# Decoder trunk on one core: part of the odd layer's input product split by token halves around the last layer norm of the even layer

## The chip, the cores and the metric

One core of a Trainium2 chip runs the whole kernel. The metric is device time in microseconds (us) of one execution. Three runs of the kernel before gave 1377.31, 1377.62 and 1377.97 us, a median of 1377.62.

## The reference

A trunk of two layers over 256 tokens of width 2048. The even layer has an SSD mixer and a block attention side by side; the odd layer is a diagonal state-space mixer (S5). After each layer the residual is normalised. What matters here is the seam between the two:

```python
x = layer_norm(DEEPNORM_ALPHA * x + h, ln_g[0], ln_b[0])   # h: output projection of the even layer
u, gate = jnp.split(x @ w_in, 2, axis=-1)                  # odd layer: 2048 -> 4096
```

Every row (token) of `x` is normalised over its 2048 features, scaled by `ln_g` and shifted by `ln_b`, and then multiplied by the input weights `in1_w` of the odd layer. All data is float32.

## The kernel before, in words

**Weights as a stream of units.** All large weight matrices are laid out as *units* of 128 partitions x 2 x 512 (256 rows of the matrix by 512 columns, 512 KB). `split_to(i)` brings units in order up to number `i`: SP issues the load of `raw`, ScalarE copies it to a rounded high part `wh` (L224), VectorE subtracts to get the low part `wl` (L226). `raw`, `wh` and `wl` have four buffers each, so a unit's split waits until the unit four places earlier has been multiplied. A product of float32 accuracy is made of three matmuls: high by high, high by low, low by high.

**Two kinds of product.** In the kind "x" (`xmm`, L264) the activations, 128 features by 128 tokens, are the stationary operand and 512 columns of weights move; the result has tokens on partitions. In the kind "w" (`wmm`, L277) 128 x 128 of weights are stationary and the activations of all 256 tokens move; the result has features on partitions. A unit of kind "w" is 2 x 4 x 3 = 24 matmuls. A product over 2048 features has eight units (`CU`), and its sums lie in two PSUM banks that `banks()` hands out in turn from two pairs.

**The even layer's output projection** is four blocks of 512 columns with 16 units each. The last block uses `product_apart`: ten units for both token halves, then the last six (`NKEEP`), whose split weights are all kept in SBUF, first for token half 0 and then for token half 1, 36 matmuls each. So half 0 is complete while PE works on half 1, and its residual and norm (`after0`) run beside that.

**The norm.** For a token half `t`, `res0` adds the residual (L950) and takes statistics (L951); `norm_stats` aggregates them (L967 to L970, with a square root on ScalarE). `step(t, i)` then handles a quarter of the features (512): two VectorE row operations (L993 and L996) give the normalised values `D`; four PE transposes (L341, `transpose4`) turn them into an auxiliary PSUM bank; ScalarE evicts the high part into tile C (L1004) and VectorE the low part into tile F (L1005). C and F are the moving operands of the odd layer's input product. Inside them the 256 token columns lie as four strips of 64, and token half `t` is 32 columns of each strip.

**Order.** A tile scheduler orders each engine's instructions when the program is built, and each engine then takes its instructions in that order; `tc.issue_after` pins an instruction behind another. `jobs` is a queue of small pieces of work that `pump` and `drain` hand out between units. In the kernel before, PE's order at the seam is: 36 matmuls for half 1; eight transposes of steps (0, 0) and (0, 1); 60 dummy matmuls of 128 x 64 by 64 columns on zeros (`warm(WARM1)`, L349); four transposes of step (1, 0); then the first input product `first1`, unit by unit, with 256 moving columns. Step (1, 1), the second quarter of half 1, is handed out before unit 1; the third quarters before unit 3; the last ones before unit 5 (`later`). VectorE's order has the low part of step (1, 0) before the row operations of the later steps, and most of those before the low parts of the later steps.

After this, seven more blocks of the input product follow on PE, beside the state-space mixer; then the GLU product, the output projection and the last norm.

Of the kernel before, what the change touches and what calls it, by code (L numbers as in the profile page):

```python
# [10 lines left out]
F32R = mybir.dt.float32r  # L11
AF = mybir.ActivationFunctionType
OP = mybir.AluOpType
# [3 lines left out]
P = 128  # L17
S = 256
D = 2048
KT = D // P  # L20
UK = 2
CU = KT // UK
ALPHA = 4.0 ** 0.25
NKEEP = 6
WARM0 = 70
WARM1 = 60
EPS = 1e-5
NEG = -1e30
SCALE = 128.0 ** -0.5
# [129 lines left out]
def trunk(tc, io, out):  # L159
    nc = tc.nc  # L160
    V, A, G, T = nc.vector, nc.scalar, nc.gpsimd, nc.tensor
# [6 lines left out]
    with ExitStack() as top:  # L168
# [18 lines left out]
        ident = C("ident")  # L187
# [4 lines left out]
        def big(tag, shape, dt=F32):  # L192
            return slot.tile(shape, dt, tag=tag, name=nm(tag))
# [4 lines left out]
        ready = {}  # L198
# [31 lines left out]
        jobs = deque()  # L230
        back = deque()
        goal = [0, 0.0]
        unit = [0]
# [12 lines left out]
        def drain():  # L246
            while jobs:
                jobs.popleft()()
# [6 lines left out]
        def banks():  # L255
            turnno[0] += 1
            return [main.tile([P, 512], F32, tag=f"m{turnno[0] % 2}{o}", name=nm("main")) for o in range(2)]

        def xmm(ps, o, wpair, j, hk, start, stop):
            (xh, xl), k = hk  # L260
            wh, wl = wpair
            sl = slice(o * P, o * P + P)
            for i, (l, r) in enumerate(((xh, wh), (xh, wl), (xl, wh))):
                T.matmul(ps[o], l[:, k, sl], r[:, j, :], start=start and i == 0, stop=stop and i == 2)  # L264

        def wmm(ps, u, nu, hl, wpair):
            pv = [p.rearrange("p (f n) -> p f n", n=S) for p in ps]
            wh, wl = wpair
            steps = [(j, o) for j in range(UK) for o in range(4)]
            if u == nu - 1:  # L270
                steps = [(j, o) for o in range(4) for j in range(UK)]
            for j, o in steps:
                first, end = u == 0 and j == 0, u == nu - 1 and j == UK - 1
                (xh, xl), k = hl(u * UK + j)
                sl = slice(o * P, o * P + P)
                for i, (l, r) in enumerate(((wh, xh), (wh, xl), (wl, xh))):
                    T.matmul(pv[o // 2][:, o % 2, :], l[:, j, sl], r[:, k, :],  # L277
                             start=first and i == 0 and o % 2 == 0, stop=end and i == 2 and o % 2 == 1,
                             skip_group_check=True)

        def product(kind, hl, nu=CU, prelude=None):
            ps = banks()
            for u in range(nu):
                if prelude:
                    prelude(u)
                split_to(unit[0] + 3)
                wpair = ready.pop(unit[0])
                if kind == "w":
                    wmm(ps, u, nu, hl, wpair)
                else:  # L290
                    last = u == nu - 1
                    steps = [(j, o) for o in range(2) for j in range(UK)] if last else [(j, o) for j in range(UK) for o in range(2)]
                    for j, o in steps:
                        xmm(ps, o, wpair, j, hl(u * UK + j), u == 0 and j == 0, last and j == UK - 1)
                unit[0] += 1
                pump(nu - 1 - u)
            return ps
# [12 lines left out]
                if lo == 0:  # L310
                    between()

        def product_apart(hl, nu, nk, after):
            ps = banks()
            for u in range(nu - nk):
                split_to(unit[0] + 3 + u)
                wpair = ready.pop(unit[0])
                for j in range(UK):
                    for o in range(2):
                        xmm(ps, o, wpair, j, hl(u * UK + j), u == 0 and j == 0, False)  # L320
                unit[0] += 1
                pump(nu - nk - 1 - u)
            drain()
            base = unit[0]
            for o in range(2):
                for i in range(nk):
                    split_to(base + i + 3)
                    u = nu - nk + i
                    for j in range(UK):
                        xmm(ps, o, ready[base + i], j, hl(u * UK + j), u == 0 and j == 0, u == nu - 1 and j == UK - 1)  # L330
                    pump(nk - 1 - i)
                after(ps, o)
                if o == 0:
                    drain()
            for i in range(nk):
                ready.pop(base + i)
            unit[0] += nk

        def transpose4(dst, srcs):
            for i, s in enumerate(srcs):  # L340
                T.transpose(dst[:, i * P : i * P + P], s, ident)  # L341

        idle = cst.tile([P, 64], F32R, name="idle")
        G.memset(idle.bitcast(F32), 0.0)
# [1 line left out]
        def warm(n):  # L346
            px = aux()
            for i in range(n):
                T.matmul(px[:64, 0:64], idle, idle, start=i == 0, stop=i == n - 1)  # L349
# [5 lines left out]
        mr0 = cst.tile([P, 2, 4], F32, name="mr0")  # L355
# [7 lines left out]
        with ExitStack() as l0:  # L363
# [136 lines left out]
            ps = product("w", xhl)  # L500
# [465 lines left out]
        def norm_stats(stt, mr, t):  # L966
            V.bn_aggr(mr[:, t, 0:2], stt[:, t, :, :].rearrange("p a b -> p (a b)"))  # L967
            V.tensor_scalar(mr[:, t, 2:3], mr[:, t, 1:2], EPS, None, op0=OP.add)
            A.activation(mr[:, t, 2:3], mr[:, t, 2:3], AF.Sqrt)
            return lambda: V.reciprocal(mr[:, t, 2:3], mr[:, t, 2:3])  # L970

        with ExitStack() as lt:
            tp = lt.enter_context(tc.tile_pool(name="tp", bufs=1))
            keep[0], keep[1] = tp, range(unit[0] + 2 * CU - NKEEP, unit[0] + 2 * CU)
            rows = [tp.tile([P, D], F32, name=f"row{i}") for i in range(2)]
            for i in range(2):
                nc.sync.dma_start(rows[i], lnrow(i))
            jobs.append(lambda ps=ps: res0(tp.tile([P, 2, 512], F32, tag="xr", name="xr2"), ps, 2, (0, 1)))
            x1n = x1[0]
            x1t = {}  # L980

            tail = {}

            def step(t, i, stats=None):
                if not x1t:
                    x1t["h"] = big("C", [P, KT, S], F32R)
                    x1t["l"] = big("F", [P, KT, S], F32R)
                sl = slice(512 * i, 512 * i + 512)
                xv = x1n[:, t, sl]
                with ExitStack() as pin:  # L990
                    if tail:
                        pin.enter_context(tc.issue_after(tail["v"].ins))
                    V.scalar_tensor_tensor(xv, xv, mr0[:, t, 0:1], rows[0][:, sl], op0=OP.subtract, op1=OP.mult)  # L993
                    if stats:
                        stats()
                    op2 = V.scalar_tensor_tensor(xv, xv, mr0[:, t, 2:3], rows[1][:, sl], op0=OP.mult, op1=OP.add)  # L996
                tail["v"] = op2
                px = aux()
                transpose4(px, [x1n[:, t, (4 * i + f) * P : (4 * i + f) * P + P] for f in range(4)])
                pv = px.rearrange("p (f c s) -> p f s c", f=4, s=4)  # L1000
                fs = slice(4 * i, 4 * i + 4)
                hv = x1t["h"][:, fs, :].rearrange("p f (s c) -> p f s c", s=4)[:, :, :, 32 * t : 32 * t + 32]
                lv = x1t["l"][:, fs, :].rearrange("p f (s c) -> p f s c", s=4)[:, :, :, 32 * t : 32 * t + 32]
                A.activation(hv, pv, AF.Copy)  # L1004
                low = V.tensor_tensor(lv, pv, hv.bitcast(F32), op=OP.subtract)  # L1005
                if (t, i) in ((0, 1), (1, 0)):
                    tail["v"] = low

            def after0(ps, t):
                def first():  # L1010
                    with ExitStack() as pin:
                        if tail:
                            pin.enter_context(tc.issue_after(tail["v"].ins))
                        res0(tp.tile([P, 2, 512], F32, tag="xr", name=nm("xr")), ps, 3, (t,))
                    step(t, 0, norm_stats(st0, mr0, t))

                jobs.append(first)
                if t == 0:
                    jobs.append(lambda: step(0, 1))

            product_apart(tailhl, 2 * CU, NKEEP, after0)
            warm(WARM1)
            drain()
            x1 = x1n

            def x1hl(k):
                return (x1t["h"], x1t["l"]), k

            later = {1: [(1, 1)], 3: [(0, 2), (1, 2)], 5: [(0, 3), (1, 3)]}
            first1 = product("w", x1hl, prelude=lambda u: [step(t, i) for t, i in later.get(u, [])])  # L1030

        ax.close()

# [249 lines left out]
```

## Time and profile before

| | us |
|---|---|
| runs (3) | 1377.31, 1377.62, 1377.97 |
| profiled execution, its own time | 1377.72 |
| its span, first to last instruction | 1375.6 |
| PE busy in the span | 1356.2 |
| mean granted TensorE clock | 0.996 of full |
| SP's and POOL's DMA, whole span | 283.14 MB, mean 206 GB/s |
| last wide matmul of the even layer starts | 865.78 |
| first matmul of the odd layer starts | 873.30 |

How to read it: times inside a profile count from the first instruction of the span. PE is TensorE's matmuls and PEld its weight loads, which overlap with matmuls; DVE is VectorE, ACT ScalarE, POOL GpSimd, SP the engine that issues most DMAs. A timeline row has the start, the duration, the engine, the line, the operation, the tiles (out<-in), the shape of the stationary operand (partitions*columns), of the moving one, and the number of instructions merged in the row; the time in brackets is how long the engine had been idle, and who ended that. Ends of matmuls are modelled, so the pace of a stream is read from starts. In a windows row stand the stretch, its length, the busy time of PE, PEld, DVE, ACT and POOL with counts, the granted clock, the DMA share and GB/s.

### The profile page before, as it was taken

How to read it: one execution, taken by the hardware profiler on the slowest of the kernel's cores; microseconds unless marked ns; L12 is line 12 of the kernel's file. 1: busy time of each engine (PE TensorE's matmuls, PEld its weight loads, DVE VectorE, ACT ScalarE, POOL GpSimd, SP SyncE). 2: the span in 40 equal slices, each digit the busy share in tenths (PEclk: the TensorE clock that was granted, in tenths of full speed). 3: DMA queues.
4: the chain of work that ended last, by engine and by line, in shares of the span. 5: the costliest groups of instructions: out<-in, count | busy, mean ns of one | idle time of the engine just before them, and what ended most of it. 6: DMA issues, size and time to landing. Idle time of an engine off the chain costs nothing.

```text
span 1375.6 us, 27155 instructions
## 1 busy us (share of the span) xinstructions
PE 1356.2 (99%) x11064; PEld 1273.4 (93%) x11064; DVE 981.8 (71%) x1556; ACT 679.5 (49%) x872; POOL 306.2 (22%) x457
## 2 busy tenths in 40 slices
PE   9999999999999999999999999999999999999996
PEld 9999999988998998998988888899999999999885
DVE  5789958777767688687768756758788846454556
ACT  5565468765544544554554435244345545444441
POOL 0258776842011011011000000023433100000001
PEclk9999999999999999999999999999999999999998
DMA  8546665445556656657656669488888665555762
GB/s 306 176 150 190 211 203 189 159 149 192 171 158 201 205 177 210 213 165 228 221 184 222 224 211 323 159 254 275 283 275 277 197 203 183 182 182 182 253 208 86
DMA packets 79212, 283.14 MB, mean 206 GB/s; under 512 B 9840, under 2 KB 10480, under 8 KB 78576
## 3 DMA queue, kind: packets, MB, share of 16 engines
q1 hardware_dynamic: 68112, 239.33, 53.8%
q0 software_dynamic: 10400, 40.90, 9.1%
q8 instruction: 86, 1.41, 0.4%
q10 hardware_dynamic: 576, 1.18, 0.2%
q14 instruction: 38, 0.31, 0.1%
HBM read 260.41 MB, written 20.97 MB: 205 GB/s over the span
## 4 chain that ended last, share of the span: by engine, by line
PE 82%; POOL 10%; DMA 3%; DVE 2%; issue 1%; ACT 1%; POOLq 0%; SPq 0%; ACTq 0%
PE main L277 50%; PE main L264 26%; POOL F L611 5%; DMA wb<-F 2%; POOL F L613 2%; POOL F L614 2%; POOL F L606 1%; PE enc L1093 1%; PE aux L677 1%; PE aux L341 1%; PE aux L349 1%; PE dec L1138 1%; PE aux L673 1%; PE aux L851 1%; PE aux L883 1%
## 5 line engine op out<-in xcount | busy, mean ns | idle before, releaser
L226 DVE TENSOR_TENSOR wl<-raw,wh 128x1024 fp32r<-128x1024 f32 x431 | 538.9, 1255 | 281.9 <-ACT wh L224 275.7
L224 ACT ACTIVATE wh<-raw 128x1024 fp32r<-128x1024 f32 x431 | 454.7, 1058 | 535.8 <-PE main L277 325.5
L277 PE MATMUL main<-A,wl 128*128 128x256 f32 x1920 | 545.5, 284 | 3.7 <-DVE wl L226 3.6
L277 PE MATMUL main<-A,wh 128*128 128x256 f32 x1920 | 548.4, 286 | 0.0
L277 PE MATMUL main<-B,wh 128*128 128x256 f32 x1920 | 544.4, 284 | 0.0
L277 PEld LDWEIGHTS main<-A,wl 128*128 128x128 f32 x1920 | 369.0, 192 | 4.6 <-DVE wl L226 4.5
L277 PEld LDWEIGHTS main<-A,wh 128*128 128x128 f32 x1920 | 369.2, 192 | 0.8 <-issue 0.2
L277 PEld LDWEIGHTS main<-B,wh 128*128 128x128 f32 x1920 | 369.3, 192 | 0.3
L277 PE MATMUL main<-C,wh 128*128 128x256 f32 x512 | 148.1, 291 | 0.7 <-ACT C L1004 0.7
L277 PE MATMUL main<-F,wh 128*128 128x256 f32 x512 | 145.4, 285 | 0.1
L277 PE MATMUL main<-C,wl 128*128 128x256 f32 x512 | 145.1, 284 | 0.0
L277 PEld LDWEIGHTS main<-C,wh 128*128 128x128 f32 x512 | 98.3, 192 | 2.9 <-ACT C L1004 0.9
L264 PE MATMUL main<-wh,A 128*128 128x512 f32 x256 | 100.7, 393 | 0.0
L264 PE MATMUL main<-wl,A 128*128 128x512 f32 x256 | 100.1, 391 | 0.0
L264 PE MATMUL main<-wh,C 128*128 128x512 f32 x256 | 100.0, 392 | 0.0
L264 PE MATMUL main<-wh,B 128*128 128x512 f32 x256 | 99.9, 390 | 0.0
L264 PE MATMUL main<-wl,C 128*128 128x512 f32 x256 | 99.8, 390 | 0.0
L264 PE MATMUL main<-wh,F 128*128 128x512 f32 x256 | 99.8, 390 | 0.0
L277 PEld LDWEIGHTS main<-F,wh 128*128 128x128 f32 x512 | 98.7, 193 | 0.4 <-DVE F L1005 0.4
L277 PEld LDWEIGHTS main<-C,wl 128*128 128x128 f32 x512 | 98.7, 193 | 0.1
L611 POOL TENSOR_TENSOR F<-F 128x16 f32<-128x16 f32 (+5 forms) x96 | 67.1, 720 | 3.8
L685 POOL DMA_DIRECT2D wb<-ob x16 | 8.8, 547 | 254.2 <-ACT ob L678 200.3
(279 smaller groups left out, 1565.2 us busy)
## 6 DMA issues: line engine op xcount, KB each, us to landing
raw<-in_wi SPq DMA_DIRECT2D x271, 512.0 KB, 4.2
raw<-in_wo SPq DMA_DIRECT2D x96, 512.0 KB, 4.2
raw<-in_wglu SPq DMA_DIRECT2D x64, 512.0 KB, 3.5
wt<-wb POOLq DMA_DIRECT2D x16, 896.0 KB, 7.6
wb<-ob POOLq DMA_DIRECT2D x16, 512.0 KB, 4.4
bc<-in_s5bc SPq DMA_DIRECT2D x16, 256.0 KB, 4.4
wb<-F POOLq DMA_DIRECT2D x16, 256.0 KB, 3.8
wb<-om POOLq DMA_DIRECT2D x16, 128.0 KB, 4.2
```

Source lines behind the costliest of these rows:

```text
L224: last["a"] = A.activation(wh, raw, AF.Copy)
L226: last["v"] = V.tensor_tensor(wl, raw, wh.bitcast(F32), op=OP.subtract)
L264: T.matmul(ps[o], l[:, k, sl], r[:, j, :], start=start and i == 0, stop=stop and i == 2)
L277: T.matmul(pv[o // 2][:, o % 2, :], l[:, j, sl], r[:, k, :], start=first and i == 0 and o % 2 == 0, stop=end and i == 2 and o % 2 == 1, sk ...
L341: T.transpose(dst[:, i * P : i * P + P], s, ident)
L349: T.matmul(px[:64, 0:64], idle, idle, start=i == 0, stop=i == n - 1)
L606: G.tensor_copy(cs[:, i, :, 1], phi[:, i, sl])
L611: G.tensor_tensor(pq[:, i, :, :, 0:m], cs[:, :, :, 1 : m + 1], cs[:, i, :, n : n + 1].unsqueeze(1).to_broadcast([P, 2, 8, m]), op=OP.mult)
L613: G.tensor_tensor(cs[:, 0, :, n + 1 : n + 1 + m], pq[:, 0, 0, :, 0:m], pq[:, 1, 1, :, 0:m], op=OP.subtract)
L614: G.tensor_tensor(cs[:, 1, :, n + 1 : n + 1 + m], pq[:, 0, 1, :, 0:m], pq[:, 1, 0, :, 0:m], op=OP.add)
L673: T.transpose(pe[:, a * P : a * P + P], ev[:, a, :], ident)
L677: T.matmul(pk[at : at + 64, a * 16 : a * 16 + 16], ev[:, a, 64 * i : 64 * i + 64], cv[:, a, i, :], start=True, stop=True)
```

## The change

The dummy matmuls at the seam go. `wmm` gets a parameter `t`: with it, a unit is multiplied by the 128 tokens of half `t` alone, so that the moving operand and the result are 4 x 32 columns. After `product_apart` the first three units (`HEAD1`) of the first input product are multiplied by half 0. Only then are the remaining jobs, with residual and norm of half 1, handed out; `first1` then multiplies the same three units by half 1 and the other five by all 256 tokens, into the same two banks. `step` is cut in two: `scaled` (the two row operations) and `turned` (transposes and evictions). `after0` hands out only the `scaled` parts of half 0; their `turned` parts are issued by `mid`, and the last six matmuls of half 1 of `product_apart` (those of the sixth kept unit) are pinned behind its last transpose. For half 1, the first `scaled` part and `turned(1, 0)` are handed out after the head; the other steps stay where they were.

In the issue order of the changed program PE has: 30 of the 36 matmuls for half 1; the eight transposes of half 0; the other six; 72 matmuls of 128 x 128 by 4 x 32 columns (the head); four transposes of step (1, 0); 72 such matmuls for half 1, with the transposes of step (1, 1) after the sixth of unit 1, those of (0, 2) before unit 2, those of (1, 2) and the first of (0, 3) after the first two matmuls of unit 2; then unit 3 with 256 columns, and the remaining transposes behind unit 4. On VectorE, between the low part of (1, 0) and that of (1, 1) stand seven row operations, the split of unit 4 and two row operations; before, it was nine row operations and that split. SP and POOL issue the same instructions in the same order.

```diff
-WARM1 = 60
+HEAD1 = 3
...
-        def wmm(ps, u, nu, hl, wpair):
+        def wmm(ps, u, nu, hl, wpair, t=None):
             pv = [p.rearrange("p (f n) -> p f n", n=S) for p in ps]
+
+            def part(x):
+                return x if t is None else x.rearrange("p (s c) -> p s c", s=4)[:, :, 32 * t : 32 * t + 32]
+
...
-                    T.matmul(pv[o // 2][:, o % 2, :], l[:, j, sl], r[:, k, :],
-                             start=first and i == 0 and o % 2 == 0, stop=end and i == 2 and o % 2 == 1,
+                    T.matmul(part(pv[o // 2][:, o % 2, :]), l[:, j, sl], part(r[:, k, :]),
+                             start=first and i == 0 and o % 2 == 0 and t != 1, stop=end and i == 2 and o % 2 == 1,
                              skip_group_check=True)
...
-        def product(kind, hl, nu=CU, prelude=None):
-            ps = banks()
+        def product(kind, hl, nu=CU, prelude=None, ps=None, head=0):
+            ps = ps or banks()
...
-                    wmm(ps, u, nu, hl, wpair)
+                    wmm(ps, u, nu, hl, wpair, 1 if u < head else None)
...
-        def product_apart(hl, nu, nk, after):
+        def product_apart(hl, nu, nk, after, mid=None):
...
-                    for j in range(UK):
-                        xmm(ps, o, ready[base + i], j, hl(u * UK + j), u == 0 and j == 0, u == nu - 1 and j == UK - 1)
+                    with ExitStack() as pin:
+                        if mid and o == 1 and i == nk - 1:
+                            pin.enter_context(tc.issue_after(mid().ins))
+                        for j in range(UK):
+                            xmm(ps, o, ready[base + i], j, hl(u * UK + j), u == 0 and j == 0, u == nu - 1 and j == UK - 1)
...
-                    step(t, 0, norm_stats(st0, mr0, t))
+                    scaled(t, 0, norm_stats(st0, mr0, t))
 
                 jobs.append(first)
-                if t == 0:
-                    jobs.append(lambda: step(0, 1))
-
-            product_apart(tailhl, 2 * CU, NKEEP, after0)
-            warm(WARM1)
+                jobs.append((lambda: turned(1, 0)) if t else (lambda: scaled(0, 1)))
+
+            def mid():
+                turned(0, 0)
+                return turned(0, 1)
...
+            product_apart(tailhl, 2 * CU, NKEEP, after0, mid)
+            ps = banks()
+            split_to(unit[0] + 3)
+            for u in range(HEAD1):
+                wmm(ps, u, CU, x1hl, ready[unit[0] + u], 0)
             drain()
...
-            first1 = product("w", x1hl, prelude=lambda u: [step(t, i) for t, i in later.get(u, [])])
+            first1 = product("w", x1hl, prelude=lambda u: [step(t, i) for t, i in later.get(u, [])], ps=ps, head=HEAD1)
```

`transpose4` now returns its last transpose; `scaled` and `turned` together hold the lines of `step` unchanged.

More of the change, by code (lines that the diff above doesn't have):

```diff
@@ L340, in transpose4 @@
             for i, s in enumerate(srcs):
-                T.transpose(dst[:, i * P : i * P + P], s, ident)
+                end = T.transpose(dst[:, i * P : i * P + P], s, ident)
+            return end
         idle = cst.tile([P, 64], F32R, name="idle")
@@ L982, in trunk, with scaled @@
             tail = {}
[L984 to L987, printed above, removed]
+            def scaled(t, i, stats=None):
                 sl = slice(512 * i, 512 * i + 512)
@@ L995, in step, with turned @@
                         stats()
-                    op2 = V.scalar_tensor_tensor(xv, xv, mr0[:, t, 2:3], rows[1][:, sl], op0=OP.mult, op1=OP.add)
-                tail["v"] = op2
+                    tail["v"] = V.scalar_tensor_tensor(xv, xv, mr0[:, t, 2:3], rows[1][:, sl], op0=OP.mult, op1=OP.add)
+            def turned(t, i):
+                if not x1t:
+                    x1t["h"] = big("C", [P, KT, S], F32R)
+                    x1t["l"] = big("F", [P, KT, S], F32R)
                 px = aux()
-                transpose4(px, [x1n[:, t, (4 * i + f) * P : (4 * i + f) * P + P] for f in range(4)])
+                end = transpose4(px, [x1n[:, t, (4 * i + f) * P : (4 * i + f) * P + P] for f in range(4)])
                 pv = px.rearrange("p (f c s) -> p f s c", f=4, s=4)
@@ L1007, in step @@
                     tail["v"] = low
+                return end
+            def step(t, i):
+                scaled(t, i)
+                turned(t, i)
             def after0(ps, t):
@@ L1014, in first, with x1hl @@
                         res0(tp.tile([P, 2, 512], F32, tag="xr", name=nm("xr")), ps, 3, (t,))
-                    step(t, 0, norm_stats(st0, mr0, t))
+                    scaled(t, 0, norm_stats(st0, mr0, t))
                 jobs.append(first)
-                if t == 0:
-                    jobs.append(lambda: step(0, 1))
-            product_apart(tailhl, 2 * CU, NKEEP, after0)
-            warm(WARM1)
+                jobs.append((lambda: turned(1, 0)) if t else (lambda: scaled(0, 1)))
+            def mid():
+                turned(0, 0)
+                return turned(0, 1)
+            def x1hl(k):
+                return (x1t["h"], x1t["l"]), k
+            product_apart(tailhl, 2 * CU, NKEEP, after0, mid)
[3 more added lines that the diff above has]
+                wmm(ps, u, CU, x1hl, ready[unit[0] + u], 0)
             drain()
             x1 = x1n
-            def x1hl(k):
-                return (x1t["h"], x1t["l"]), k
             later = {1: [(1, 1)], 3: [(0, 2), (1, 2)], 5: [(0, 3), (1, 3)]}
-            first1 = product("w", x1hl, prelude=lambda u: [step(t, i) for t, i in later.get(u, [])])
+            first1 = product("w", x1hl, prelude=lambda u: [step(t, i) for t, i in later.get(u, [])], ps=ps, head=HEAD1)
         ax.close()
```

## The prediction

> **What bounds the kernel now.** I read the page first, then the chain of work that ended last in order of time, then the PE timeline around the layer norm between the layers. All times are microseconds from the span's start; line numbers are those of the kernel before.
>
> ```profile
> span 1375.6 us, 27155 instructions
> PE 1356.2 (99%) x11064; PEld 1273.4 (93%) x11064; DVE 981.8 (71%) x1556; ACT 679.5 (49%) x872; POOL 306.2 (22%) x457
> PE 82%; POOL 10%; DMA 3%; DVE 2%; issue 1%; ACT 1%; POOLq 0%; SPq 0%; ACTq 0%
> ```
>
> TensorE is the bound. The chain shows where it is not:
>
> ```profile
> 867.28 1.29 DVE F L1005 x2
> 871.15 0.76 DVE D L996
> 874.03 4.40 PE main L277 x24
> 883.04 8.39 PE main L277 x70
> ...
> 1366.08 2.19 DVE D L1256 x3
> ```
>
> At the layer norm the chain leaves PE for DVE, and from 874.03 it stays on PE until 1366. So what delays PE here delays the end by as much, and what is saved is saved. The PE timeline of this stretch:
>
> ```profile
> 865.78 0.39 PE L264 MATMUL main<-wh,B 128*128 128x512 f32 x1
> 866.02 1.03 PE L341 MATMUL aux<-consts,D 128*128 128x128 f32 x8
> 866.81 3.72 PE L349 MATMUL aux<-idle 128*64 128x64 f32 x60
> 871.96 0.66 PE L341 MATMUL aux<-consts,D 128*128 128x128 f32 x4 [1.44 <-DVE D L996]
> 873.30 0.62 PE L277 MATMUL main<-C,wh 128*128 128x256 f32 x2 [0.69 <-ACT C L1004]
> 874.03 0.58 PE L277 MATMUL main<-F,wh 128*128 128x256 f32 x1
> 874.41 0.42 PE L277 MATMUL main<-C,wl 128*128 128x256 f32 x1
> ...
> 877.20 0.28 PE L277 MATMUL main<-C,wl 128*128 128x256 f32 x1
> ...
> 878.14 0.28 PE L277 MATMUL main<-F,wh 128*128 128x256 f32 x1
> ...
> 882.80 0.36 PE L277 MATMUL main<-F,wh 128*128 128x256 f32 x1
> 883.00 0.28 PE L277 MATMUL main<-C,wl 128*128 128x256 f32 x1
> ```
>
> The last useful matmul starts at 865.78 and the next at 873.30: 7.5 us with twelve transposes and sixty dummy matmuls. Starts, not durations, give the pace, since neighbours overlap: eight steps from 877.20 to 878.14 are 118 ns each; at 874.41 a matmul took twice that. The windows view says why (the column after POOL is the granted clock):
>
> ```profile
> 870.00:872.00 2.00, 0.56 (x10) 0.45 (x8) 1.83 (x5) 0.20 (x1) 0.00 (x0) 1.00 0.00 0
> 872.00:874.00 2.00, 1.24 (x6) 0.70 (x6) 0.72 (x2) 0.60 (x1) 0.00 (x0) 0.88 0.00 0
> 874.00:877.00 3.00, 2.97 (x14) 2.98 (x15) 2.93 (x5) 0.00 (x0) 0.00 (x0) 0.51 0.00 0
> 877.00:882.00 5.00, 5.00 (x45) 5.00 (x45) 4.93 (x7) 2.09 (x3) 0.00 (x0) 1.00 0.01 3
> ```
>
> The clock was half for about 3.4 us (0.48 us before 874 and 2.94 after). Some 2.8 us at half pace lost about 1.4 us. In all, before, unit 3 begins at 883.00 + 21 x 0.12 = 885.5 (the 22 left of unit 2 run from 882.80). That is the mark I compare with.
>
> **The change part by part.** It puts 72 matmuls of 128 columns (units 0 to 2, first token half) where the dummies were, and turns the 72 later ones of 256 columns into 72 of 128. The question is what a matmul of 128 columns costs. No row shows this one, so I look at weight loads:
>
> ```profile
> L349 PEld LDWEIGHTS aux<-idle x130: 137/227/227, 0.9 to 870.3; 128*64 128x64 f32 x130
> L692 PEld LDWEIGHTS aux<-kt,consts x48: 187/192/192, 458.9 to 816.8; 128*128 128x128 f32 x48
> 459.06 0.83 PE L692 MATMUL aux<-kt,consts 128*128 128x128 f32 x6
> 459.64 0.36 PE L277 MATMUL main<-A,wh 128*128 128x256 f32 x1
> 459.84 0.28 PE L277 MATMUL main<-B,wh 128*128 128x256 f32 x1
> 817.16 49.02 PE main L264 x216
> ```
>
> A 64-column load takes 137 ns, a 128-column one 192: 55 ns per 64 columns, so 110 ns of loading per full matmul beside a fixed part that overlaps. The dummies agree: sixty from 866.81, the last at 870.3, are 59 ns each for 64 weight columns and only 64 moving ones, and twice 59 is 118. Six of L692, 128 by 128, take (459.84 - 0.12 - 459.06) / 6 = 110 ns. So pace is set by the 128 weight columns as long as few columns move: **110 ns** (L692) to **120 ns** (the 256-column matmul when DMAs run) per half-width matmul. I take 118, the 256-column row, because it has the same operands, weights and DMA-quiet stretch. The far end on the cheap side is a line through 227 ns for 512 columns (49.02 / 216) and 120 for 256: 67 ns for 128; that is a rival below. That the moving part is four strips of 32 columns I cost at nothing: moving 128 columns needs some 53 ns by that line's slope, so even at twice that it hides under the load; without that cover it would add 72 x 2 times the excess.
>
> The other rows that the walk needs:
>
> ```profile
> 863.69 0.75 DVE L996 SCALAR_TENSOR_TENSOR D<-D,mr,row 128x512 f32<-128x512 f32 x1
> 868.49 0.68 DVE L950 SCALAR_TENSOR_TENSOR D<-xr,main 128x512 f32<-128x512 f32 x1
> 873.28 0.69 DVE L1005 TENSOR_TENSOR F<-aux,C 128x512 fp32r<-128x512 f32 x1 [1.38 <-ACT C L1004]
> 873.89 0.74 DVE L993 SCALAR_TENSOR_TENSOR D<-D,mr,row 128x512 f32<-128x512 f32 x1
> 879.02 0.75 DVE L996 SCALAR_TENSOR_TENSOR D<-D,mr,row 128x512 f32<-128x512 f32 x1
> 880.35 1.22 DVE L226 TENSOR_TENSOR wl<-raw,wh 128x1024 fp32r<-128x1024 f32 x1
> 881.48 0.69 DVE L1005 TENSOR_TENSOR F<-aux,C 128x512 fp32r<-128x512 f32 x1
> ```
>
> Transposes of the first half, now ahead of the last six wide matmuls: PE reaches them at 866.02 - 6 x 0.227 = 864.66, and their input is ready at 863.69 + 0.75 = 864.44, so nothing waits. The eight take about 0.87 (8 x 0.109, from 1.03 for eight with one 0.27 tail). The six wide ones then end where the transposes ended: the head starts at **866.9**. Its low parts are ready: L1005 began 1.26 after the transposes (867.28 against 866.02), so the first is done by 866.6. Gain: the eviction hides under matmuls.
>
> Second half's residual and norm on DVE: they follow those two L1005, so they move 1.3 us earlier, from 868.49 to about 867.2. The added wait of L950 on the last wide matmul (about 867.1) costs nothing beside that; behind it are only the norm's own operations. The scaled rows end about 870.6 in place of 871.9. **This gain goes nowhere**, since in the changed issue order their transposes stand behind the whole head on PE, whose queue is in order: 866.9 + 72 x 0.118 = **875.4** (T). Before, it was 871.96.
>
> From T the old chain repeats: evictions, then the third matmul 2.07 after T (874.03 - 871.96), DVE's next row operation 1.93 after T (873.89). The DVE order in the changed program: seven row operations (873.89 to 879.02, 5.13), L226 for unit 4 (881.48 - 880.35 = 1.13), two row operations (880.35 - 879.02 = 1.33), then the low part that unit 2's third matmul needs (0.69). It is there at T + 1.93 + 5.13 + 1.13 + 1.33 + 0.69 + 0.06 = T + 10.3. PE gets to it sooner: 2.07 + 48 x 0.118 + 13 transposes x 0.109 = T + 9.2, so it waits 1.1. The other 22 of unit 2 take 2.6, and unit 3 begins at T + 12.9 = **888.3**. Three transposes that before had been done by then remain: 0.33.
>
> Sum: 888.3 + 0.33 - 885.5 = **+3.1 us**. The second pass costs as much as the old full one, and the first pass is 8.5 us in a gap that had 5.1 left for it. Each nanosecond of pace moves it by 0.094 us (72 + 22 matmuls): +2.3 at 110, +3.3 at 120. The regained clock (1.4) is in it.
>
> Costed at nothing: the sixty dummies go into the head's place; SP and POOL issue the same transfers in the same order, and the weights of the first units lie ready (all queues quiet here, 0 to 3 GB/s in the windows rows); the accumulators taken earlier are the pair idle since the block before; ACT's split of unit 4 waits for unit 0's second pass (about T + 5) and L226 comes at T + 7, so two microseconds cover it. If that cover went, L226 and the low part behind it would be late one for one.
>
> Made against the profiled execution, 1377.72 (span 1375.6 plus 2.1 around it; the median of the runs is 1377.62): 1377.72 + 3.1 = **1380.8**.
>
> **Rivals.**
> *Gate closes once.* PE is idle for 0.9 and 0.5 after T and for 1.1 before unit 2. Before, a window with 0.56 + 1.24 busy in 4 us closed the clock; here the window round the late wait is two thirds busy. Price as before: some 1.4, so 1382.2. The Trainium skill ("TensorE: Matmul & The Clock Gate", section "What's actually happening") says that about one idle window of 3.4 us halves the clock; the 3.4 us above agree, and a wait of 1.1 alone wouldn't do.
> *Gate closes in the half-width passes.* They move columns under half of the time. The kernel's opening speaks for it:
>
> ```profile
> 0.94 7.67 PE L349 MATMUL aux<-idle 128*64 128x64 f32 x70 [0.94 <-POOL idle L344]
> 8.43 0.56 PE L277 MATMUL main<-A,wh 128*128 128x256 f32 x1
> ```
>
> Seventy dummies at 107 ns, half pace, for 7.5 us never freed the clock. Against it: the sixty kept it at 866.8 to 870.3, and these use all 128 weight columns. From 873.5 on, 86 matmuls cost 0.095 more each and 17 transposes 0.109, a late opening 1.4 as above, and the wait of 1.1 goes: 3.1 + 8.2 + 1.9 + 1.4 - 1.1 = +13.5, about 1391.
> *Not slower: weight loads don't bind.* If loads overlap one another, the pace is that of the moving columns, 67 ns, on PE in both passes. Then T is 871.7, DVE's chain still ends at T + 10.3, and the end is 94 x 0.051 = 4.8 earlier than forecast: -1.7, 1376.0. It decides below 85 ns. Against it stand L692's 110 and the dummies' 59. The Trainium skill's section "Back-to-back issue gap" on the same page gives 81 ns for a sustained pair of load and 128-column matmul; by it, as an estimate, the time would be -0.4, 1377.3. No run here shows that pace.
> *The head doesn't fill the gap* (issued elsewhere): the issue order shows it between the wide matmuls and the second half's transposes, so I give this next to nothing.
>
> **How the numbers follow.** Within 0.2% means 2.8 us, about what a measurement of this kernel tells from no change. Forecast 0.55: between +2.3 and +3.3, over 2.8 from 115 ns on, so 0.35 slower and 0.20 within. Gate once 0.18, slower. Gate in the passes 0.09, slower. Loads not binding 0.12, within. Anything else 0.06: 0.05 faster, 0.01 within. That is 0.62 slower, 0.33 within, 0.05 faster. The range reaches from 1377.2 (half of the not-slower rival) to 1382.9 (gate once, with its spread), leaving out the +13 and the rest.
>
> **What would show it.** Head matmuls 110 to 120 ns apart and the second half's transposes near 875.4; the second pass at the same pace; one wait of about 1 us on DVE's low part before unit 2's third matmul; granted clock 1.00 from 866 to 885; unit 3 near 888. A pace under 85 ns, half clock within the passes, or the transposes before 873 would make it wrong.

## The result and the profile after

The changed kernel takes **1386.34 us** (median of 17 runs, 1379.44 to 1391.66) against 1377.62 for the kernel before (17 runs beside them, 1375.29 to 1381.21): ratio 1.006, 95% interval 1.0049 to 1.007. It is slower by 0.6%; +3.1 us was forecast and +8.7 came. The spread is part of the result: the kernel before varies by 6 us, the changed one by 12, and its time goes with the mean granted clock of the run: 1379.4 to 1381.4 us at 0.996 to 0.997 (three runs), 1384.8 to 1386.6 at 0.991 or 0.992 (eight), 1388.1 to 1391.7 at 0.988 to 0.990 (six). The profiled execution is one of the mild ones, 1381.42 us at 0.996. Two of the experiments below had one disturbed run each (6641 us in fill_first, 1458 us in head_of_one), which the ranges given there leave out and which move their medians by 0.02 us.

What the mean clock is made of matters for this. All traces show half clock in the last 30 us of the kernel, for some 6 to 9 us. That costs no PE time, since the last matmul is done by then (in the changed kernel 7.4 us of it run from 1372.0 to the end, with no PE instruction). So about 0.997 is what a run without any loss at the seam has, and one closed stretch of 3.4 us more takes off 0.0012. At the median run's 0.991, half clock lasted about 2 x 0.009 x 1386 = 25 us, and 16 to 19 us of it stood elsewhere than at the end: an estimate, as that run has no trace.

The page after, its first lines and the shares of the chain:

```profile
span 1379.4 us, 27179 instructions
PE 1360.1 (99%) x11076; PEld 1277.2 (93%) x11076; DVE 981.8 (71%) x1556; ACT 679.0 (49%) x872; POOL 306.0 (22%) x457
PE 81%; POOL 10%; DMA 4%; DVE 2%; issue 1%; ACT 1%; POOLq 0%; SPq 0%; ACTq 0%
```

The work of DVE, ACT and POOL is the same; PE has 3.9 us more. The PE timeline of the changed kernel at the seam (the matmul of the "w" kind is now L281, the transposes L348):

```profile
864.04 1.03 PE L348 MATMUL aux<-consts,D 128*128 128x128 f32 x8
864.83 0.48 PE L264 MATMUL main<-wh,A 128*128 128x512 f32 x1
...
866.29 0.34 PE L281 MATMUL main<-C,wh 128*128 128x128 f32 x2
866.46 0.27 PE L281 MATMUL main<-F,wh 128*128 128x128 f32 x1
...
874.28 0.62 PE L348 MATMUL aux<-consts,D 128*128 128x128 f32 x4
875.59 0.44 PE L281 MATMUL main<-C,wh 128*128 128x128 f32 x2 [0.69 <-ACT C L1013]
876.31 0.33 PE L281 MATMUL main<-F,wh 128*128 128x128 f32 x1 [0.28 <-DVE F L1014]
...
884.38 0.33 PE L281 MATMUL main<-F,wh 128*128 128x128 f32 x1 [0.87 <-DVE F L1014]
...
886.22 0.34 PE L281 MATMUL main<-C,wh 128*128 128x128 f32 x1
886.36 0.41 PE L281 MATMUL main<-F,wh 128*128 128x128 f32 x1
886.58 0.41 PE L281 MATMUL main<-C,wl 128*128 128x128 f32 x1
...
889.67 0.30 PE L281 MATMUL main<-F,wh 128*128 128x256 f32 x1
889.81 0.28 PE L281 MATMUL main<-C,wl 128*128 128x256 f32 x1
```

This execution reached the seam 0.6 us earlier than the profiled one before (864.04 against the 864.66 forecast for the moved transposes), so times are compared from there. The head runs without a gap at (874.28 - 866.29) / 72 = 111 ns. Behind the second half's transposes come the two waits known from before, and before unit 2 the forecast wait on DVE's low part. Then, at 886.3, the pace drops to 214 ns, and it returns at 889.8. The windows view names it:

```profile
870.00:874.00 4.00, 4.00 (x38) 4.00 (x38) 0.00 (x0) 0.00 (x0) 0.00 (x0) 1.00 0.00 0
874.00:877.00 3.00, 2.03 (x16) 1.65 (x16) 1.40 (x3) 0.60 (x1) 0.00 (x0) 1.00 0.00 0
...
880.00:885.00 5.00, 4.10 (x37) 3.69 (x35) 5.00 (x8) 2.65 (x5) 0.00 (x0) 1.00 0.30 97
885.00:890.00 5.00, 5.00 (x32) 5.00 (x32) 3.55 (x4) 1.06 (x1) 2.87 (x8) 0.66 0.56 203
```

The granted clock (behind the POOL column) falls only after the later wait, for 0.34 x 5 / 0.5 = 3.4 us. Below, "the gate closes" means that the granted clock goes to half, and "opens" that it returns to full. This is the mild case; the experiments had to show what the other fourteen runs do.

### The profile page after: what moved, and what is told of

It is laid out like the page before. It is cut to its first block, busy times and chain, and to the rows that moved or that the text cites. A ratio compares the mean times of both kernels' runs of the same rounds, so it can differ in the third digit from the quotient of the medians.

```text
span 1379.4 us, 27179 instructions
## 1 busy us (share of the span) xinstructions
PE 1360.1 (99%) x11076; PEld 1277.2 (93%) x11076; DVE 981.8 (71%) x1556; ACT 679.0 (49%) x872; POOL 306.0 (22%) x457
## 4 chain that ended last, share of the span: by engine, by line
PE 81%; POOL 10%; DMA 4%; DVE 2%; issue 1%; ACT 1%; POOLq 0%; SPq 0%; ACTq 0%
PE main L281 49%; PE main L264 25%; POOL F L619 5%; DMA wb<-F 2%; POOL F L621 2%; POOL F L622 2%; PE enc L1112 1%; PE aux L685 1%; POOL F L614 1%; DVE wl L226 1%; PE aux L357 1%; PE dec L1157 1%; DMA um<-ud 1%; PE aux L348 1%; PE aux L681 1%
## 5 line engine op out<-in xcount | busy, mean ns | idle before, releaser
L281 PE MATMUL main<-A,wl 128*128 128x256 f32 x1920 | 545.3, 284 | 3.5 <-DVE wl L226 3.5
L281 PE MATMUL main<-A,wh 128*128 128x256 f32 x1920 | 548.2, 286 | 0.0
L281 PE MATMUL main<-B,wh 128*128 128x256 f32 x1920 | 544.3, 283 | 0.0
L281 PEld LDWEIGHTS main<-A,wl 128*128 128x128 f32 x1920 | 368.8, 192 | 4.3 <-DVE wl L226 4.1
L281 PEld LDWEIGHTS main<-A,wh 128*128 128x128 f32 x1920 | 369.1, 192 | 0.8 <-issue 0.2
L281 PEld LDWEIGHTS main<-B,wh 128*128 128x128 f32 x1920 | 369.0, 192 | 0.3
L281 PE MATMUL main<-C,wh 128*128 128x256 f32 (+1 forms) x536 | 154.5, 290 | 0.7 <-ACT C L1013 0.7
L281 PE MATMUL main<-F,wh 128*128 128x256 f32 (+1 forms) x536 | 151.9, 284 | 1.2 <-DVE F L1014 1.2
L281 PE MATMUL main<-C,wl 128*128 128x256 f32 (+1 forms) x536 | 151.5, 283 | 0.0
L281 PEld LDWEIGHTS main<-C,wh 128*128 128x128 f32 x536 | 103.1, 193 | 2.9 <-ACT C L1013 0.9
L281 PEld LDWEIGHTS main<-F,wh 128*128 128x128 f32 x536 | 103.6, 193 | 1.6 <-DVE F L1014 1.5
L281 PEld LDWEIGHTS main<-C,wl 128*128 128x128 f32 x536 | 103.4, 193 | 0.1
```

The costliest lines, as they stand in the source:

```text
L281: T.matmul(part(pv[o // 2][:, o % 2, :]), l[:, j, sl], part(r[:, k, :]), start=first and i == 0 and o % 2 == 0 and t != 1, stop=end and i ...
```

## The experiments

The theory at the start was that half-width matmuls (those that move 128 columns) alone close the clock gate; the rival, that PE's waits close it. All medians stand beside runs of the kernel before on the same chip. "Seam to end" is, in a trace, from the first transposes of half 0 to the end of the span: 1375.6 - 866.02 + 1.36 = 510.9 before (its transposes come six wide matmuls later), 1379.4 - 864.04 = 515.4 in the changed kernel.

| experiment | median us (range) | before on that chip | ratio, 95% interval | mean clock of its runs |
|---|---|---|---|---|
| again | 1384.66 (1381.98 to 1387.51) | 1377.94 | 1.0051, 1.0034 to 1.0068 | 0.990 to 0.996 |
| dense_both | 1378.84 (1376.36 to 1380.65) | 1377.94 | 1.0004, 0.9995 to 1.0014 | 0.996 to 0.997 |
| head_only | 1377.90 (1376.08 to 1379.88) | 1377.94 | 0.9999, 0.9989 to 1.0008 | 0.995 to 0.997 |
| dense_head | 1380.74 (1377.87 to 1385.71) | 1377.94 | 1.0024, 1.0010 to 1.0039 | 0.990 to 0.998 |
| filled | 1379.14 (1377.56 to 1380.33) | 1377.37 | 1.0008, 0.9999 to 1.0017 | 0.995 to 0.998 |
| long_head | 1402.90 (1401.65 to 1404.00) | 1377.37 | 1.0179, 1.0162 to 1.0195 | 0.996 to 0.997 |
| busy_gap | 1373.81 (1372.97 to 1374.80) | 1377.37 | 0.9972, 0.9960 to 0.9983 | 0.997 |
| before_busy | 1375.38 (1373.68 to 1376.98) | 1377.37 | 0.9983, 0.9974 to 0.9992 | 0.995 to 0.998 |
| fill_first | 1377.60 (1375.83 to 1379.28) | 1377.98 | 0.9990, 0.9981 to 0.9999 | 0.996 to 0.997 |
| fill_second | 1386.28 (1382.05 to 1389.01) | 1377.98 | 1.0052, 1.0038 to 1.0066 | 0.990 to 0.996 |
| head_of_one | 1378.03 (1374.08 to 1378.95) | 1377.98 | 0.9995, 0.9986 to 1.0003 | 0.992 to 0.996 |
| again_2 | 1383.34 (1381.60 to 1387.97) | 1377.98 | 1.0039, 1.0028 to 1.0050 | 0.991 to 0.995, one run 0.943 |

**again and again_2**: the changed kernel itself, no edit.

> The changed kernel once more, for a trace of a typical run (the one profiled took 1381.42 us at a mean clock of 0.996; most of its runs took 1385 to 1390 at 0.988 to 0.992). Theory 1, half-width passes: matmuls of 128 columns move data under half of the time, the clock gate takes such windows of 3.4 us for idle, and most runs have two to six windows at half clock between the head's start and some microseconds after unit 3. Then the trace shows the granted clock near 0.5 while PE is busy without a gap, inside the head or the second pass, and the median is again about 1386. Theory 2, waits: the gate closes after PE's own waits (1.3 us after the second half's transposes, 0.9 us before unit 2). Then the head, which has no gap, runs at full clock in every run, and half clock begins only behind a wait.

> The changed kernel once more, for a trace of a typical run. With waits and half-width matmuls together as the cause, a run of 1384 to 1390 shows half clock from a window boundary behind the second half's transposes until a full window of 256-column matmuls has passed, 7 to 17 us later, and the head before it at full clock.

The medians came back, 5 to 7 us above before, but both profiled executions were mild ones again (1381.98 and 1381.84 us): the head at full clock, half clock only behind the wait before unit 2. So no typical run was traced. The clock also orders these runs less sharply than those of the result: again has 1383.42 and 1385.44 us at the same 0.995, and one run of again_2 is given as 0.943 at 1382.10 us, which stays unexplained. In again_2's trace the half clock lasted longer, 6.8 us or two stretches of 3.4, with the second pass's end and unit 3 inside:

```profile
880.00:885.00 5.00, 4.10 (x36) 3.69 (x35) 5.00 (x7) 2.06 (x4) 0.02 (x1) 1.00 0.32 105
885.00:890.00 5.00, 5.00 (x26) 5.00 (x26) 2.82 (x4) 1.06 (x1) 2.85 (x8) 0.52 0.70 257
890.00:895.00 5.00, 5.00 (x36) 5.00 (x36) 1.23 (x1) 1.06 (x1) 0.00 (x0) 0.80 1.02 426
```

**dense_both, head_only, dense_head**: which of the two passes has to be half-width. In all three the head's place and count stay. With 256 columns it moves the even layer's tiles, and it is pinned behind the last wide matmul.

```diff
 # dense_both and dense_head: the head
-wmm(ps, u, CU, x1hl, ready[unit[0] + u], 0)
+wmm(ps, u, CU, lambda k: ((yah, yal), k), ready[unit[0] + u])
 # dense_both and head_only: the later product starts afresh, 256 columns
-first1 = product("w", x1hl, prelude=..., ps=ps, head=HEAD1)
+first1 = product("w", x1hl, prelude=..., ps=ps)
```

> The head's 72 matmuls move 256 columns of the even layer's tiles in place of 4 x 32 of half 0, so they are pure cover: the later product starts its sums afresh and runs with 256 columns in all units. Weights, count, place and all waits stay; only the moved columns double, in both passes. By the paces known (111 ns at 128 columns, 120 at 256) the work is 94 x 0.009 = 0.8 us more than in the change. Theory 1: the gate stays open, mean clock 0.996 or above, runs within 4 us of each other, median about 1381 (before +3.3). Theory 2: as in the change, median about 1386 and clock about 0.991.

> The head with 4 x 32 columns as in the change, its sums thrown away: the later product starts afresh with 256 columns in all units. Theory 1: the gate can close in the head but opens one to two windows into the second pass: median 1381 to 1385, between the doubly dense one and the change. Theory 2: about 1386, as the waits are the same.

> The head with 256 columns of other data, then the second pass with 4 x 32 columns of half 1 added on top: the first 512 columns of the odd layer's input product are therefore not the reference's. Theory 1: full clock in the head; the second pass is 10 us long and half-width, so the gate can still close in it: median 1382 to 1386, clock 0.991 to 0.995. Theory 2: about 1386.

With a second pass of 256 columns the loss is gone, whatever the head moves: 1378.8 and 1377.9. Neither theory had forecast as little (1381 for dense_both and 1381 to 1385 for head_only by the first, about 1386 for both by the second). With a half-width second pass behind a dense head it is there in half of the runs: six at 0.996 to 0.998 take 1377.9 to 1379.3, six at 0.990 to 0.994 take 1382.2 to 1385.7; of the changed kernel's first 17 runs it was 14. head_only keeps the waits behind its transposes, 0.7 and 0.2 us (the expectations call this first wait 1.3 us, which is the time from the start of the transposes to the next matmul; PE's idle time in the changed kernel is 0.7 + 0.3 = 1.0 us). Its clock stays up:

```profile
873.00:876.00 3.00, 2.09 (x16) 1.65 (x16) 1.12 (x2) 0.60 (x1) 0.00 (x0) 1.00 0.00 0
876.00:880.00 4.00, 4.00 (x36) 4.00 (x35) 3.89 (x7) 1.06 (x1) 0.00 (x0) 1.00 0.02 4
```

So waits of this size alone don't do it; in the kernel before, a longer one did, with 1.80 us busy in 4. dense_head's trace is the first of a bad run (1385.22 us):

```profile
874.00:877.00 3.00, 2.03 (x16) 1.65 (x16) 1.41 (x3) 0.60 (x1) 0.00 (x0) 1.00 0.00 0
877.00:880.00 3.00, 3.00 (x23) 3.00 (x23) 2.77 (x4) 0.91 (x1) 0.00 (x0) 0.76 0.02 5
880.00:885.00 5.00, 5.00 (x26) 5.00 (x26) 4.51 (x6) 0.76 (x3) 0.00 (x0) 0.50 0.32 105
885.00:890.00 5.00, 5.00 (x26) 5.00 (x26) 3.12 (x4) 2.21 (x3) 0.09 (x1) 0.50 0.31 100
890.00:895.00 5.00, 5.00 (x25) 5.00 (x25) 1.23 (x1) 1.06 (x1) 2.78 (x8) 0.50 0.72 264
895.00:900.00 5.00, 5.00 (x43) 5.00 (x41) 1.83 (x2) 1.88 (x3) 0.00 (x0) 0.93 1.01 415
```

Half clock starts in the second pass, two microseconds behind the wait, and lasts through it, although PE is busy without a gap (5.00 of 5.00). Two of these kernels differ from the change in one thing more: in dense_both and head_only the scheduler put two row operations fewer ahead of DVE's low part, and PE doesn't wait before unit 2, where the change has 0.9 us. In dense_head's traced run that wait is gone too, as PE runs at half pace. The later experiments separate the waits.

**long_head**: is a half-width stream without waits enough? The head runs four times, and its sums are thrown away.

```diff
-for u in range(HEAD1):
+for v in range(4 * HEAD1):
+    u = v % HEAD1
     wmm(ps, u, CU, x1hl, ready[unit[0] + u], 0)
...
-first1 = product("w", x1hl, prelude=..., ps=ps, head=HEAD1)
+first1 = product("w", x1hl, prelude=..., ps=ps)
```

> The head run four times (288 half-width matmuls without a wait, 32 us or nine windows of the gate at 111 ns), its sums thrown away; the later product starts afresh with 256 columns, as in the kernel with the head alone (1377.9). Theory 1a: the gate closes inside the stream after one to three windows and stays closed, so that the pace goes to 213 ns: 1410 to 1425. Theory 1b: full clock and 111 ns throughout, 1377.9 + 216 x 0.111 = 1402, runs within 4 us.

Its windows, and the line of its chain for the head:

```profile
870.00:880.00 10.00, 10.00 (x92) 10.00 (x91) 1.79 (x5) 0.20 (x1) 0.00 (x0) 1.00 0.01 2
880.00:890.00 10.00, 10.00 (x92) 10.00 (x92) 0.00 (x0) 0.00 (x0) 0.00 (x0) 1.00 0.00 0
890.00:900.00 10.00, 10.00 (x92) 10.00 (x91) 0.00 (x0) 0.00 (x0) 0.00 (x0) 1.00 0.01 2
```

```profile
868.39 32.11 PE main L281 x288
```

The clock stays full for 32 us; 32.11 / 288 = 111.5 ns. By the count of matmuls the time is 1377.9 (head_only) + 216 x 0.1115 = 1402.0, and 1402.9 came. **The theory that half-width matmuls alone close the gate falls.** What is left is that half-width matmuls and a wait must fall together, for waits as short as these.

**filled, fill_first, fill_second**: the change with its waits filled by half-width dummies, both, the first alone, the second alone.

```diff
+def busy(n, m):
+    px = aux()
+    w = ready[unit[0]][0]
+    for i in range(n):
+        T.matmul(px[:, 0:m], w[:, i % UK, 0:P], yah[:, i % KT, 0:m], start=i == 0, stop=i == n - 1)
 drain()
+busy(14, P)                                     # filled, fill_first
...
-prelude=lambda u: [step(t, i) for t, i in later.get(u, [])]
+prelude=lambda u: [...] + [busy(9, P) for _ in range(u == 2)]   # filled, fill_second
```

> The changed kernel with its two waits in the second pass filled by half-width dummies: 14 matmuls of 128 x 128 by 128 columns behind the second half's first transposes, 9 before unit 2. Order of all else as in the change. Theory 1a (half-width matmuls alone close the gate): as the change, 1384 to 1386, clock 0.990 to 0.994. Theory 1b (a window closes the gate only if half-width matmuls and a wait fall together in it, and then half-width matmuls can't open it again): no wait longer than 0.3 us is left, so the gate stays open: 1379 to 1380, clock 0.997.

> The change with only the first wait of the second pass filled: 14 half-width dummies behind the second half's first transposes; the wait before unit 2 stays. If the first wait closes the gate in most runs and the half-width second pass keeps it closed (8 us at least, since the stream of half-width matmuls doesn't open it), then this takes most of the loss away: about 1380, clock 0.996, with at most one closing after the later wait. If the later wait is what costs, it stays at 1384 to 1386.

> The change with only the second wait filled: 9 half-width dummies before unit 2, and the 1.3 us behind the second half's first transposes stay open. If the first wait closes the gate: 1383 to 1386, clock 0.991 to 0.994. If the later one does: about 1379.5.

Filling the first wait takes the whole loss away: 1377.6, and all its runs lie at 0.996 or above. Filling only the second leaves it: 1386.3. On the same chip that is 8.7 us between the two, as much as the change lost. So the first wait with half-width matmuls around it is enough for the loss. In fill_first the wait before unit 2 is nearly gone too, as its dummies delay PE (PE 4.91 busy of 5.00 from 880 to 885), so the second wait was not tried alone with the first one filled. fill_second's trace (1389.01 us) shows a bad run of what is otherwise the change:

```profile
870.00:874.00 4.00, 4.00 (x38) 4.00 (x37) 0.27 (x1) 0.00 (x0) 0.00 (x0) 1.00 0.00 0
874.00:877.00 3.00, 2.03 (x16) 1.65 (x14) 1.08 (x2) 0.60 (x1) 0.00 (x0) 0.94 0.00 0
877.00:880.00 3.00, 3.00 (x16) 3.00 (x15) 2.93 (x5) 0.00 (x0) 0.00 (x0) 0.50 0.02 5
880.00:885.00 5.00, 5.00 (x26) 5.00 (x25) 4.00 (x6) 1.65 (x2) 0.00 (x0) 0.50 0.08 13
885.00:890.00 5.00, 5.00 (x25) 5.00 (x25) 2.62 (x4) 1.06 (x1) 2.89 (x7) 0.50 0.52 186
890.00:895.00 5.00, 5.00 (x26) 5.00 (x26) 0.00 (x0) 0.58 (x1) 0.94 (x2) 0.50 0.96 373
895.00:900.00 5.00, 5.00 (x35) 5.00 (x35) 2.42 (x3) 2.11 (x4) 0.00 (x0) 0.79 1.02 420
```

```profile
889.65 0.42 PE L281 MATMUL main<-F,wh 128*128 128x128 f32 x1
889.86 0.42 PE L281 MATMUL main<-C,wl 128*128 128x128 f32 x1
...
894.34 1.93 PE L348 MATMUL aux<-consts,D 128*128 128x128 f32 x8
895.92 0.56 PE L281 MATMUL main<-C,wh 128*128 128x256 f32 x1
```

Half clock lasts from about 876.6 (0.06 x 3 / 0.5 = 0.4 us before 877) to 897.1 (0.21 x 5 / 0.5 = 2.1 us after 895), 20.5 us or six times 3.4. The half-width matmuls then come 213 ns apart. The second pass ends at 894.3, and the clock returns 2.8 us later, behind eight transposes and 1.2 us of 256-column matmuls. Seam to end is 1386.9 - 864.39 = 522.5, against 1377.2 - 865.56 = 511.6 in fill_first.

**busy_gap, before_busy**: what the seam is worth without a head, and what the dummies of before are worth.

```diff
 # busy_gap: HEAD1 = 0; busy(n) is n matmuls of 256 columns of the even layer's tile A
+busy(34)
 drain()
+busy(9)
...
 # before_busy: the kernel before
-warm(WARM1)
+busy(42)
 drain()
+busy(9)
```

> The part of the change without the head: half 0's transposes ahead of the last six wide matmuls, and in the gap 34 dummies of 256 columns before the second half's transposes and 9 behind them. Units 0 to 2 are multiplied once, with 256 columns. By the rows of before the transposes of half 1 come 1 us earlier and the half clock is gone (1.5 to 3 us): 1374 to 1376, clock 0.997. If the clock does not matter and only order does: 1376.5 to 1377.

> The kernel before with nothing changed but its dummies: 42 of 128 x 128 by 256 columns in place of 60 of 128 x 64 by 64, and 9 more behind the second half's first transposes. The gate's share of the kernel before by itself: if the dummies of before don't count as work for the gate, the clock rises from 0.994 to 0.997 and the time falls by 1.5 to 3 us, to 1375 to 1376.5; if they do, 1377.5 to 1378.

In busy_gap the transposes of half 0 stay ahead of the last six wide matmuls, as in the change. It beats both kernels: 1373.8, 3.6 us below before (ratio 0.9972) and the narrowest range of all. before_busy alone takes 2.0 of that. The rest goes with the earlier transposes of half 0, the main thing in which the two still differ; it was not tried alone. The seam of busy_gap:

```profile
865.24 4.24 PE L1049 MATMUL aux<-A,wh 128*128 128x256 f32 x34
869.32 0.60 PE L348 MATMUL aux<-consts,D 128*128 128x128 f32 x4
869.67 1.31 PE L1049 MATMUL aux<-A,wh 128*128 128x256 f32 x9
870.82 0.40 PE L281 MATMUL main<-C,wh 128*128 128x256 f32 x2
```

PE hardly stops (0.1 us from 864 to 874), and seam to end is 1370.9 - 863.00 = 507.9.

**head_of_one**: HEAD1 = 1 in place of 3.

> The change with a head of one unit in place of three (HEAD1 = 1): 24 half-width matmuls take 2.7 us of the gap of 4 us, the second half's transposes come as early as its norm allows, and only 24 half-width matmuls follow, then 256 columns. Work: about 2 us less than the change. Gate: PE waits more in the gap but dense matmuls open it within one window: 1375.5 to 1378, clock 0.995 to 0.997. If half-width matmuls after a wait cost in proportion to their number: a third of the change's loss, about 1379.

1378.0, no better than before. PE waits 0.9 us for DVE before the second half's transposes and 0.7 behind them, and the clock is at half over three windows, from about 869 to 879:

```profile
866.00:870.00 4.00, 2.38 (x15) 1.81 (x15) 2.56 (x6) 0.80 (x2) 0.00 (x0) 0.85 0.00 0
870.00:874.00 4.00, 4.00 (x20) 4.00 (x20) 3.90 (x6) 0.00 (x0) 0.00 (x0) 0.50 0.00 0
874.00:877.00 3.00, 3.00 (x15) 3.00 (x15) 2.96 (x5) 1.66 (x2) 0.00 (x0) 0.50 0.00 0
877.00:880.00 3.00, 3.00 (x20) 3.00 (x19) 1.62 (x3) 0.00 (x0) 1.26 (x4) 0.66 0.51 162
```

The expectation that dense matmuls would open it within one window missed: 24 half-width ones stand before them at half clock, from 869 to 874.6.

## Why the prediction was wrong

- **The sign and the order of work were right.** The head's pace is 111 ns, inside the forecast 110 to 120. It hardly depends on how many columns move (111 ns with 128, 118 with 256), as it should where the weight load sets it, and it is far from the 67 of the not-slower rival. The second half's transposes start 10.2 us after those of half 0 (forecast 10.7), the waits behind them are 0.7 and 0.3 us, and the wait before unit 2 is 0.9 (forecast 1.1). The early end of the second half's norm bought nothing: DVE then idles 5.6 us.
- **The size of the work was about right.** The mild trace is 515.4 - 510.9 = 4.5 us longer from seam to end, with some 1.6 us (16 matmuls at 0.21 in place of 0.11 to 0.12) of a closed gate in it that the forecast sum left out; 2.9 is left, and at 111 ns the forecast gives 3.1 - 94 x 0.007 = 2.4. The runs with the waits filled lie -0.4 (fill_first) and +1.8 (filled) from before. A kernel before with an open gate is 2.0 faster (before_busy), so that they are +1.6 and +3.8 from it, where the forecast with its regained 1.4 taken out gives 2.4 + 1.4 = 3.8.
- **The step that failed is the clock**: "granted clock 1.00 from 866 to 885", and, in the first gate rival, "here the window round the late wait is two thirds busy" as a reason against. The sum takes the regained clock (1.4) as a gain and counts no loss. But the gate closed behind the late wait even in the mild traces, for 3.4 or 6.8 us, which is that rival's case (1382.2; these runs took 1381.4 to 1382.0). The typical run loses more, and at the earlier wait: in fill_second half clock begins at 876.6, behind the second half's first transposes, and lasts 20.5 us. With that wait filled the time is 1377.6, with it open 1386.3.
- **Why it went unseen.** The reason against it went by PE's busy share, but a half-width stream is busy to the full in the profile at either clock (10.00 of 10.00 us in long_head, 5.00 of 5.00 in fill_second). The prediction also priced the two ways the gate could close apart: a wait at +1.4 more (0.18) and half-width passes at +13.5 in all (0.09). Here both act at once, and the cost lies between them: the first wait, 1.0 us among half-width matmuls, closes the gate in most runs, and the rest of the half-width second pass never opens it. fill_first against fill_second shows the first; long_head and head_only show that half-width matmuls alone, and waits with a 256-column second pass, don't bring the loss. That the gate goes by how much PE moves in a stretch fits these runs, but how it counts was not measured.
- **The traces taken were lucky ones.** In all three traced executions of the change the clock is 1.00 from 866 to 885, as forecast. Only the times and mean clocks of the other runs, and fill_second and dense_head, show that this is not the usual case.
- **The range failed with it.** Its upper end was the single closing; a typical run has, by its mean clock, about 16 to 19 us at half clock (the estimate above), some five times as much. Nor was the variation from run to run weighed, which the three narrow runs of before didn't show: 29 of them in the experiments spread over 6 us.
- Not settled: no execution of the changed kernel itself with 1385 us or more was traced; fill_second and dense_head stand for it. That the phase of the gate's windows decides between mild and bad runs fits the traces (half clock lasts about whole multiples of 3.4 us, and begins anywhere from 876.6 to 886.3), but it is not shown, and the traces don't agree on it. Counted back from 886.3 in steps of 3.41, a boundary in the mild trace falls at 876.1 and parts the two pieces of the first wait, while in fill_second it falls at 876.6, behind both. But in dense_head, where half clock begins at 878.6, it falls at 875.2, inside the first piece, and the gate closes all the same.

## What to carry to other kernels

A matmul with 128 stationary float32 columns cost 111 ns here with 128 moving columns and 118 with 256. So splitting 256 moving columns into two passes of 128 nearly doubles the price, and work put into a gap in this way saves almost nothing later. What PE ran around a wait decided the clock: filling the wait kept it up, with half-width dummies in fill_first and with 256-column ones in busy_gap. Look at the granted clock in the windows view, not at PE's busy share, and check it by the pace: at the opening of the kernel before, the column reads 1.00, while 256-column matmuls start 213 ns apart from 9 to 13 us.

```profile
8.00:14.00 6.00, 6.00 (x34) 6.00 (x34) 4.07 (x6) 4.09 (x6) 0.00 (x0) 1.00 1.03 405
```

And when times spread, sort them by granted clock before trusting one trace.

## What the runs showed of the hardware that was not expected

- Half-width matmuls (128 by 128 columns, 111 ns apart) held an open gate for 32 us (long_head), but didn't open a closed one: with no gap of PE it stayed at half through 17 us of them (fill_second, 877 to 894).
- A stretch that PE is busy for two thirds (2.03 of 3.00 us) can close the gate, if what it runs is half-width. With a 256-column second pass nearly the same wait (2.09 of 3.00) left it open in head_only's trace, and no run of it shows the loss (mean clock 0.997 in eight of twelve, 0.995 at the lowest). The Trainium skill ("TensorE: Matmul & The Clock Gate", section "What's actually happening") speaks of idle windows; the 3.4 us fit (half clock lasts 3.4, 6.8 or 20.5 us), the condition is wider here.
- The 60 small dummies of the kernel before cost it 2.0 us against 42 of 256 columns in their place and nine more behind the second half's transposes (ratio 0.9983, 0.9974 to 0.9992).
